# Loads issued from two hardware queues instead of one, in a NaN-ignoring row maximum

## The chip, the cores and the metric

The kernel runs on one core of a Trainium2 chip. The metric is the device time of the whole program in microseconds (us). Every run told here was of the fast state: executions of one kernel agree within 0.3% for the kernel before, and within about 1% for most of the kernels with late loads that follow. Ratios are the mean time of one kernel's fast runs over the mean of the other's in the same rounds on the same chip, so they are not quite the ratios of the medians that are quoted.

## The reference

```python
def setup_inputs():
    batch, seq, dim = 32, 2048, 2048
    x = np.random.randn(batch, seq, dim).astype(np.float32)
    mask = np.random.rand(batch, seq, dim) < 0.1
    x[mask] = np.nan
    return {"x": x, "axis": -1}

def reference(x, axis):
    return np.nanmax(x, axis=axis).astype(np.float32)
```

The input is 537 MB and each element is needed once; the output is 0.26 MB.

## The kernel before

Each of the 128 partitions takes its share of the 65,536 rows. A tile holds seven rows of 2048 floats per partition, 7 MB in all, and there are three tile buffers. ScalarE turns the upper half of each float into a 16-bit key in which NaN sorts low (a "piece" of two or three rows), GpSimd turns the key back and writes it into the tile, and VectorE takes the maximum. Once in three tiles ScalarE itself does the turning back for the last piece, to relieve GpSimd; this is called the write-back here. A negative number in the piece list marks it.

```python
TILES = (
    [([1], [1], [1])]
    + [
        ([7], [2, 3, 2], [2, 3, 2]),      # loads, pieces, reduces
        ([7], [2, 3, 2], [2, 3, 2]),
        ([7], [2, 3, -2], [2, 3, 2]),     # -2: write-back by ScalarE
    ] * 19
    + ...                                 # cut: the last tiles, in smaller and smaller loads
)
...
    io = ctx.enter_context(tc.tile_pool(name="io", bufs=3))
    mid = ctx.enter_context(tc.tile_pool(name="mid", bufs=3))
...
        for loads, pieces, reds in g:
            xt = io.tile([P, WIDE * D], i32, tag="xt")
            at = 0
            for c in loads:
                nc.sync.dma_start(                       # every load on SyncE's queue
                    out=xt[:, at * D : (at + c) * D],
                    in_=xg[:, (base + at) * D : (base + at + c) * D],
                )
                at += c
            ...
            for c in pieces:
                ...
                nc.scalar.activation(out=kp, in_=xp.bitcast(i16)[:, 1::2], func=ACT.Prelu, ...)
                if back:
                    nc.scalar.activation(out=xp.bitcast(i16)[:, 1::2], in_=kp, func=ACT.Copy, ...)
                else:
                    nc.gpsimd.tensor_scalar(out=xp.bitcast(i16)[:, 1::2], in0=kp, ...)
                ...
                    nc.vector.tensor_reduce(out=acc[...], in_=xt[...], op=ALU.max, ...)
```

The program is written in the order of the data. A scheduler then decides the order in which the instructions of each engine stand, and puts in the waits. The order on ScalarE is the scheduler's, unless it is pinned.

Of the kernel before, what the change touches and what calls it, by code (L numbers as in the profile page):

```python
# [1 line left out]

# [4 lines left out]
# [9 lines that stand above are left out]
        ([7], [2, 3, -2], [2, 3, 2]),  # L17
    ] * 19
    + [([7], [2, 3, 2], [2, 3, 2])] * 2
    + [([1, 6], [-1, 3, 1, -2], [4, 3])]  # L20
    + [([7], [3, 2, -2], [3, 4])]
    + [([7], [2, 2, 3], [2, 2, 3])] * 2
    + [([7], [2, 1, 2, 2], [2, 1, 2, 2])]
    + [([5, 2], [1, 1, 1, 2, -1, 1], [1, 1, 1, 3, 1])]
    + [([3, 4], [2, -1, 2, 2], [3, 2, 2])] * 2
    + [([3, 4], [2, -1, 1, 1, 2], [3, 2, 2])]
    + [([3, 2, 2], [1, 2, 1, -1, 1, 1], [1, 4, 2])]
    + [([3, 2, 2], [2, 1, 1, -1, 1, 1], [2, 1, 2, 2])]
    + [([2, 1, 2, 2], [1, 1, 1, 1, -1, 1, 1], [2, 3, 1, 1])]
    + [([2, 1, 1, 1, 2], [1, 1, 1, 1, -1, 1, 1], [1, 1, 1, 2, 1, 1])]  # L30
    + [([1, 1, 1, 1, 1, 1, 1], [1, 1, 1, -1, 1, 1, -1], [1, 1, 2, 1, 1, 1])]
)

GROUPS = [TILES[:14]] + [TILES[i : i + 12] for i in range(14, 74, 12)]
WIDE = 7

KEYS = 3



TOP = 0x7F7F
NAN = 0x7FC0
LOW = -129

EDGE = TOP + 0.25

NONE = -255.0 * 2.0**120


@with_exitstack  # L50
def kernel(
    ctx: ExitStack,
    tc: tile.TileContext,
    x: bass.AP,
    axis: bass.AP,
    out: bass.AP,
):









    nc = tc.nc
    P = nc.NUM_PARTITIONS
    f32, i32 = mybir.dt.float32, mybir.dt.int32
    i16, u16 = mybir.dt.int16, mybir.dt.uint16  # L70
    ALU = mybir.AluOpType
    ACT = mybir.ActivationFunctionType

    nd = len(x.shape)
    assert axis in (-1, nd - 1), axis
    D = x.shape[-1]

    xr = x.bitcast(i32).flatten_outer_dims()
    R = xr.shape[0]
    of = out.bitcast(i32).flatten_outer_dims().rearrange("r c -> (r c)")  # L80
    rows = [sum(sum(loads) for loads, _, _ in g) for g in GROUPS]
    assert R == P * sum(rows)

    io = ctx.enter_context(tc.tile_pool(name="io", bufs=3))
    mid = ctx.enter_context(tc.tile_pool(name="mid", bufs=3))
    res = ctx.enter_context(tc.tile_pool(name="res", bufs=1))
    sing = ctx.enter_context(tc.tile_pool(name="sing", bufs=1))
    flag = ctx.enter_context(
        tc.tile_pool(name="flag", bufs=2, space=bass.MemoryType.PSUM)
    )  # L90
    top = sing.tile([P, 1], f32)
    nc.vector.memset(top, EDGE)  # L92
    warm = sing.tile([P, 1], f32)
    nc.scalar.activation(out=warm, in_=top, func=ACT.Prelu, alpha=0.5)  # L94

    stores = []
    used = KEYS
    r0 = 0
    for s, g in zip(rows, GROUPS):
        xg = xr[r0 : r0 + P * s].rearrange("(p s) d -> p (s d)", p=P)  # L100
        og = of[r0 : r0 + P * s].rearrange("(p s) -> p s", p=P)
        r0 += P * s
        acc = res.tile([P, s], f32, tag=f"acc{len(stores)}")
        base = 0
        for loads, pieces, reds in g:
            assert sum(loads) == sum(abs(c) for c in pieces) == sum(reds)
            xt = io.tile([P, WIDE * D], i32, tag="xt")
            at = 0
            for c in loads:
                nc.sync.dma_start(  # L110
                    out=xt[:, at * D : (at + c) * D],
                    in_=xg[:, (base + at) * D : (base + at + c) * D],
                )
                at += c
            at = done = 0
            reds = list(reds)
            for c in pieces:
                back, c = c < 0, abs(c)
                xp = xt[:, at * D : (at + c) * D]
                if used + c > KEYS:  # L120
                    kt = mid.tile([P, KEYS * D], u16, tag="kt")
                    used = 0
                kp = kt[:, used * D : (used + c) * D]
                used += c
                nc.scalar.activation(  # L125
                    out=kp,
                    in_=xp.bitcast(i16)[:, 1::2],
                    func=ACT.Prelu,
                    bias=top,
                    scale=-1.0,  # L130
                    alpha=float(TOP - LOW) / (EDGE - NAN),
                )
                if back:
                    nc.scalar.activation(  # L134
                        out=xp.bitcast(i16)[:, 1::2],
                        in_=kp,
                        func=ACT.Copy,
                        bias=float(TOP),
                        scale=-1.0,
                    )  # L140
                else:
                    nc.gpsimd.tensor_scalar(  # L142
                        out=xp.bitcast(i16)[:, 1::2],
                        in0=kp,
                        scalar1=-1.0,
                        scalar2=float(TOP),
                        op0=ALU.mult,
                        op1=ALU.add,
                    )
                at += c  # L150
                while reds and done + reds[0] <= at:
                    n = reds.pop(0)
                    nc.vector.tensor_reduce(  # L153
                        out=acc[:, base + done : base + done + n],
                        in_=xt[:, done * D : (done + n) * D]
                        .bitcast(f32)
                        .rearrange("p (c d) -> p c d", c=n),
                        axis=mybir.AxisListType.X,
                        op=ALU.max,
                    )  # L160
                    done += n
            base += at
        none = flag.tile([P, s], i32, tag="none")
        nc.vector.tensor_scalar(  # L164
            out=none,
            in0=acc,
            scalar1=NONE,
            scalar2=float(0x00C00000),
            op0=ALU.is_equal,
            op1=ALU.mult,  # L170
        )
        bits = acc.bitcast(i32)
        nc.vector.tensor_tensor(out=bits, in0=bits, in1=none, op=ALU.bitwise_or)  # L173
        stores.append(dict(out=og, in_=bits))
    for st in stores:
        nc.sync.dma_start(**st)


# [1 line left out]
_INS = ['x', 'axis']  # L180
_OUTS = [((32, 2048), 'float32')]

_NUMBERS = {'axis': -1}


# [26 lines left out]
```

## Time and profile before

In the profile lines DVE is VectorE, ACT is ScalarE, POOL is GpSimd; SPq and ACTq are the sequencers of SyncE and ScalarE, which read the engine's instructions in order and issue its loads. L125 is line 125 of the kernel; q1 is SyncE's DMA queue and q10 ScalarE's. A load has *landed* when its semaphore, the counter that other instructions wait for, says that all of it has arrived.

| | before |
|---|---|
| time, median of 3 runs | 1261.39 us (1261.24 to 1261.41) |
| span of the profiled run | 1259.5 us |
| share of the DMA engines' span that SyncE's queue takes | 98.9% |
| one 7 MB tile, landing to landing | 16.9 us |

From the page of before: busy times, the rows of 40 equal slices for the DMA engines (tenths busy, and GB/s moved), the queue table and the chain of work that ended last.

```profile
span 1259.5 us, 1258 instructions
DVE 1115.2 (89%) x242; ACT 1053.3 (84%) x281; POOL 1091.2 (87%) x219
...
DMA  9999999999999999999999999999999999999995
GB/s 412 437 437 437 437 424 421 437 438 437 435 433 435 417 435 437 437 435 435 435 426 424 437 437 434 435 435 436 419 433 437 433 438 435 420 432 429 427 425 214
...
q1 hardware_dynamic: 14688, 537.14, 98.9%
...
DMA 29%; POOL 27%; ACT 20%; issue 17%; DVE 7%; SPq 0%; ACTq 0%; POOLq 0%; DVEq 0%
```

The three compute engines are 84 to 89% busy, but the queue is busy 98.9% of the span. The chain of waits, with its 29% of DMA, does not show this at once: it walks through compute, as the load at its steps was let go by a reduce. The queue row does.

The timeline of before in the middle of the run (columns: start, duration, engine, line, operation, count, and in brackets the idle time before it with what ended it):

```profile
605.12 8.74 DVE L153 TENSOR_REDUCE acc<-xt 128x2 f32<-128x4096 f32 x2
609.56 17.15 SPq L110 DMA_DIRECT2D xt<-in_x_dram  x2
...
616.04 12.62 ACT L125 ACTIVATE kt<-xt,top 128x4096 uint16<-128x4096 int16 x3 [4.33 <-DMA xt<-in_x_dram]
628.69 4.76 ACT L134 ACTIVATE xt<-kt 128x4096 int16<-128x4096 uint16 x1
...
633.32 3.68 ACT L125 ACTIVATE kt<-xt,top 128x4096 uint16<-128x4096 int16 x1
```

The load at 609.56 goes out when VectorE is done with an old tile, 6.5 us before the tile ahead of it lands (616.04, where ScalarE begins). That distance is called the load's **lead**: the landing of the load ahead of it, less its own issue. In before the lead is 6 us or more in every one of the 58 large loads of the steady part. The write-back at 628.69 stands ahead of the next tile's first piece at 633.32.

What SyncE's sequencer waited for in before (waiter, what it waited for, total us, times, longest us):

```profile
SPq L110 <- DVE acc L153: 1072.0, 66, 27.0
```

SyncE has nothing else to do, so these 1072 us of waiting cost nothing.

### The profile page before, as it was taken

To read this page: it belongs to the slowest core of one execution; us is meant where nothing else is said; L and a number is where in the kernel's file an instruction comes from. 1 tells how busy PE (TensorE), PEld (TensorE's weight loads), DVE (VectorE), ACT (ScalarE), POOL (GpSimd) and SP (SyncE) were. 2 spreads that over 40 slices of the span, in tenths; PEclk is the share of its full clock that TensorE was granted. 3 is DMA by queue.
4 is the path that set the end of the run, shared out by engine and by line. 5 is a ranking of instruction groups with operands and counts; after the bars stand their busy time and mean duration, and the time that the engine had idled before them with its cause. 6 is when DMAs were issued, how large, how long until landed. Compare 5 with 4: busy or idle time off the path is not lost.

```text
span 1259.5 us, 1258 instructions
## 1 busy us (share of the span) xinstructions
DVE 1115.2 (89%) x242; ACT 1053.3 (84%) x281; POOL 1091.2 (87%) x219
## 2 busy tenths in 40 slices
DVE  0888898888899898888989888999888889999999
ACT  4788797887888878878888788797887899799997
POOL 2989989889898898898988989889889896999996
DMA  9999999999999999999999999999999999999995
GB/s 412 437 437 437 437 424 421 437 438 437 435 433 435 417 435 437 437 435 435 435 426 424 437 437 434 435 435 436 419 433 437 433 438 435 420 432 429 427 425 214
DMA packets 14697, 537.21 MB, mean 427 GB/s; under 512 B 2400, under 2 KB 2400, under 8 KB 2400
## 3 DMA queue, kind: packets, MB, share of 16 engines
q1 hardware_dynamic: 14688, 537.14, 98.9%
q14 instruction: 9, 0.07, 0.0%
HBM read 536.87 MB, written 0.26 MB: 426 GB/s over the span
## 4 chain that ended last, share of the span: by engine, by line
DMA 29%; POOL 27%; ACT 20%; issue 17%; DVE 7%; SPq 0%; ACTq 0%; POOLq 0%; DVEq 0%
DMA xt<-in_x_dram 29%; POOL xt L142 27%; ACT kt L125 16%; DVE acc L153 7%; ACT xt L134 4%; SPq L110 0%; DVE none L164 0%; DVE acc L173 0%; ACTq L125 0%; POOLq L142 0%; DVEq L153 0%; ACTq L134 0%
## 5 line engine op out<-in xcount | busy, mean ns | idle before, releaser
L153 DVE TENSOR_REDUCE acc<-xt 128x2 f32<-128x4096 f32 (+2 forms) x229 | 1112.6, 4916 | 140.0 <-POOL xt L142 140.0
L142 POOL TENSOR_SCALAR xt<-kt 128x4096 int16<-128x4096 uint16 (+2 forms) x215 | 1091.0, 5074 | 159.1 <-ACT kt L125 146.7
L125 ACT ACTIVATE kt<-xt,top 128x4096 uint16<-128x4096 int16 (+2 forms) x247 | 927.9, 3821 | 196.7 <-DMA xt<-in_x_dram 196.5
L134 ACT ACTIVATE xt<-kt 128x4096 int16<-128x4096 uint16 (+1 forms) x32 | 127.5, 3983 | 1.0
L94 ACT ACT_TABLE_LOAD x1 | 1.3, 1283 | 0.7 <-PEq L193 0.7
L164 DVE TENSOR_SCALAR none<-acc 128x84 int32<-128x84 f32 (+1 forms) x6 | 1.5, 251 | 0.2
L173 DVE TENSOR_TENSOR acc<-acc,none 128x84 int32<-128x84 int32 (+1 forms) x6 | 1.5, 243 | 0.2
L92 DVE MEMSET top<- 128x1 f32 x1 | 0.1, 59 | 0.8 <-PEq L193 0.8
L193 POOL MEMSET const-float32-0.0<- 128x1 f32 x1 | 0.1, 99 | 0.2 <-issue 0.2
L94 ACT ACTIVATE warm<-top 128x1 f32<-128x1 f32 x1 | 0.2, 203 | 0.0
L193 POOL MEMSET const-uint8-127<- 128x1 uint8 x1 | 0.1, 103 | 0.0
L193 POOL MEMSET const-bfloat16-1.0<- 128x1 bf16 x1 | 0.1, 102 | 0.0
L193 POOL MEMSET const-float32-1.0<- 128x1 f32 x1 | 0.1, 99 | 0.0
## 6 DMA issues: line engine op xcount, KB each, us to landing
xt<-in_x_dram SPq DMA_DIRECT2D x63, 7168.0 KB, 23.5
xt<-in_x_dram SPq DMA_DIRECT2D x10, 2048.0 KB, 25.3
xt<-in_x_dram SPq DMA_DIRECT2D x5, 3072.0 KB, 16.1
xt<-in_x_dram SPq DMA_DIRECT2D x13, 1024.0 KB, 23.2
xt<-in_x_dram SPq DMA_DIRECT2D x3, 4096.0 KB, 25.1
xt<-in_x_dram SPq DMA_DIRECT2D x1, 6144.0 KB, 23.3
xt<-in_x_dram SPq DMA_DIRECT2D x1, 5120.0 KB, 18.5
out_dram<-acc SPq DMA_DIRECT2D x5, 42.0 KB, 10.7
```

The source lines that it names most:

```text
L92: nc.vector.memset(top, EDGE)
L94: nc.scalar.activation(out=warm, in_=top, func=ACT.Prelu, alpha=0.5)
L125: nc.scalar.activation(out=kp, in_=xp.bitcast(i16)[:, 1::2], func=ACT.Prelu, bias=top, scale=-1.0, alpha=float(TOP - LOW) / (EDGE - NAN),)
L134: nc.scalar.activation(out=xp.bitcast(i16)[:, 1::2], in_=kp, func=ACT.Copy, bias=float(TOP), scale=-1.0,)
L142: nc.gpsimd.tensor_scalar(out=xp.bitcast(i16)[:, 1::2], in0=kp, scalar1=-1.0, scalar2=float(TOP), op0=ALU.mult, op1=ALU.add,)
L153: nc.vector.tensor_reduce(out=acc[:, base + done : base + done + n], in_=xt[:, done * D : (done + n) * D] .bitcast(f32) .rearrange("p (c d ...
L164: nc.vector.tensor_scalar(out=none, in0=acc, scalar1=NONE, scalar2=float(0x00C00000), op0=ALU.is_equal, op1=ALU.mult,)
L173: nc.vector.tensor_tensor(out=bits, in0=bits, in1=none, op=ALU.bitwise_or)
L193: nc = _bacc.Bacc("TRN2", target_bir_lowering=False, num_devices=1)
```

## The change

Its intent: issue whole-tile loads in turn from SyncE's and ScalarE's queues, two tiles ahead of the work, so that two transfers can be in flight from two issuers.

```diff
+    ahead = []
+    ...                                   # cut: the list of all tiles' loads
+    ready = []
+    queues = [nc.sync, nc.scalar]
+
+    def fetch():
+        xg, base, loads = ahead.pop(0)
+        xt = io.tile([P, WIDE * D], i32, tag="xt")
+        queue = queues[0]
+        if len(loads) == 1:
+            queues.reverse()
+        at = 0
+        for c in loads:
+            queue.dma_start(
+                out=xt[:, at * D : (at + c) * D],
+                in_=xg[:, (base + at) * D : (base + at + c) * D],
+            )
+            at += c
+        ready.append(xt)
...
         for loads, pieces, reds in g:
-            xt = io.tile([P, WIDE * D], i32, tag="xt")
-            at = 0
-            for c in loads:
-                nc.sync.dma_start(...)
-                at += c
+            while len(ready) < 3 and ahead:
+                fetch()
+            xt = ready.pop(0)
```

Buffers, bytes and compute are the same. In the built program 32 loads stand in ScalarE's instruction stream. Over six tiles, with T8 to T13 as the example, that stream reads (L11 is the load of tile 11):

```
T8 p1 p2 p3 | T9 p1 p2 p3 | T10 p1 | L11 | T9 write-back | T10 p2 p3 | T11 p1 p2 p3 | L13 |
T12 p1 p2 p3 | T13 p1 | T12 write-back | T13 p2 p3 | L15 | ...
```

The scheduler has also moved the write-back behind the next tile's first piece.

More of the change, by code (lines that the diff above doesn't have):

```diff
@@ L94 @@
     nc.scalar.activation(out=warm, in_=top, func=ACT.Prelu, alpha=0.5)
+    ahead = []
+    r0 = 0
+    for s, g in zip(rows, GROUPS):
+        xg = xr[r0 : r0 + P * s].rearrange("(p s) d -> p (s d)", p=P)
+        r0 += P * s
+        base = 0
+        for loads, _, _ in g:
+            ahead.append((xg, base, loads))
+            base += sum(loads)
+    ready = []
[14 more added lines that the diff above has]
+        ready.append(xt)
     stores = []
@@ L99 @@
     for s, g in zip(rows, GROUPS):
-        xg = xr[r0 : r0 + P * s].rearrange("(p s) d -> p (s d)", p=P)
         og = of[r0 : r0 + P * s].rearrange("(p s) -> p s", p=P)
@@ L106 @@
             assert sum(loads) == sum(abs(c) for c in pieces) == sum(reds)
-            xt = io.tile([P, WIDE * D], i32, tag="xt")
-            at = 0
-            for c in loads:
-                nc.sync.dma_start(
-                    out=xt[:, at * D : (at + c) * D],
-                    in_=xg[:, (base + at) * D : (base + at + c) * D],
-                )
-                at += c
+            while len(ready) < 3 and ahead:
+                fetch()
+            xt = ready.pop(0)
             at = done = 0
```

## The prediction

> **What bounds it now.** The loads. The queue table of the page gives SyncE's queue 98.9% of the 16 DMA engines' span. A 7 MB tile takes 16.8 us at the 437 GB/s of the undisturbed slices. Engines have slack per 16.8 us tile (busy times of the page over 73 full tiles' worth): VectorE 15.2, GpSimd 14.9, ScalarE 14.4. By the timeline at 599-616 us, the load of tile n+2 is issued at 609.6, when VectorE has finished tile n-1 (three buffers), 10.5 us after ScalarE began tile n and 6.5 us before tile n+1 lands. So there is always a transfer behind the current one. A fresh load costs about 2.3 us besides its transfer (first load: 4.7 us from issue to landing, 2.4 of them transfer). The ceiling of any better issue is small: 1261 less 1229 of transfer, 3 at the start and about 15 at the end leaves some 12 us, 1%.
>
> **What changes.** Bytes, compute and buffers stay; 32 of the loads move to ScalarE's stream. "Two tiles ahead" is not new: SyncE already stood at the next free buffer. The Trainium skill ("DMA: Bandwidth & Descriptors", Issuing engines are not separate DMA queues) says that both queues run on the same 16 engines and interleave; the trace agrees in that one queue already fills them. Issue itself is 0.33 us on SyncE's sequencer: nothing to save.
>
> What it adds is order. SyncE's sequencer stood idle until the buffer came free; ScalarE's reaches a load only after the ScalarE instructions ahead of it have had their waits. In the trace a semaphore instruction of ScalarE's sequencer fires at once when the previous ACTIVATE's wait is met, even if that ACTIVATE starts 4.6 us later, so a load stands behind waits, not behind execution. The built order repeats every six tiles, three ScalarE loads:
> - one behind the first piece of the next tile, so issued only when that tile has landed and the DMA engines have nothing left: idle 2.4 us;
> - one behind a whole tile: on time;
> - one behind another tile's three pieces and behind a delayed write-back; that write-back (4.77 us on ScalarE) now stands after the next tile's first piece, so VectorE frees that buffer 5 to 9 us late. The same delay hits the SyncE load after it.
>
> Walking six tiles by hand with durations of the trace (ScalarE 3.70/5.40/4.77, GpSimd 4.77/7.04, VectorE 4.41/6.55, DMA 16.8+2.3 us, both queues sharing equally) gives idle DMA of about 2.4+0.4+0.7+2.3 us: a period of 106.5 instead of 101 us. Ten such periods: +56 us. Start (first tile shares with the second, the third load waits behind it) and end: +3 us. Stores issued earlier save nothing: the last one closes the chain. All of it is on the critical path, as the DMA bounds.
>
> **Predicted: 1320 us, range 1292 to 1352.** Faster by over 2%: 0.01; within 2%: 0.10; slower: 0.89.
>
> **Right if** the DMA row shows gaps of 2 to 3 us repeating every six tiles (mean 400 to 415 GB/s, queues' sum about 94%), two queues of similar share; mean durations of ACTIVATE, TENSOR_SCALAR and TENSOR_REDUCE unchanged; ScalarE's idle time before L147's pieces for DMA grows; SyncE waits for VectorE as before; ScalarE's queue shows waits for VectorE. The chain of waits gets a larger DMA share.
>
> **Wrong if** ScalarE's sequencer does stall until the ACTIVATEs ahead have executed: then the first load of each period is 3.7 us later, the third 4.4 us, and the time is nearer 1385. Or if sharing lets the older load finish first or if the engines' slack closes the gaps: then under 1286. If two queues moved more than 437 GB/s together, it would be faster; the trace gives no sign of it. Equal sharing by itself delays a landing but wastes no bandwidth, so it should not matter.

## The result, and the profile after

| | before | after |
|---|---|---|
| time, median of 4 runs | 1261.4 us | 1352.8 us (1348.07 to 1360.45) |
| ratio, 95% interval | | 1.073 (1.067 to 1.079) |
| span of the profiled run | 1259.5 us | 1346.5 us |
| queues' share of the DMA engines' span | 98.9% | 53.0% + 41.4% = 94.4% |

The change is 7.3% slower. The forecast of "slower" was right; 1352.8 lies just outside the range of 1292 to 1352, and the loss is 91 us where 59 were predicted.

The same parts of the page, after:

```profile
span 1346.5 us, 1217 instructions
DVE 1116.8 (83%) x242; ACT 1053.4 (78%) x281; POOL 1090.0 (81%) x219
...
DMA  9999999999999989999998999998999999899995
GB/s 413 436 395 424 404 378 422 414 372 421 392 382 400 426 370 374 426 402 385 409 385 356 434 429 390 382 434 356 407 412 407 376 414 434 350 428 428 428 427 236
...
q1 hardware_dynamic: 10080, 302.26, 53.0%
q10 hardware_dynamic: 4608, 234.88, 41.4%
...
DMA 53%; ACT 21%; DVE 11%; POOL 9%; issue 5%; SPq 0%; ACTq 0%; DVEq 0%
```

Busy times of the compute engines have not moved; the rate has fallen to 350 to 436 GB/s. The chain of waits is now 53% DMA.

The timeline of after, around one of the ScalarE loads that stand behind the next tile's first piece:

```profile
514.07 3.71 ACT L147 ACTIVATE kt<-xt,top 128x4096 uint16<-128x4096 int16 x1 [4.59 <-DMA xt<-in_x_dram]
514.10 0.33 ACTq L117 DMA_DIRECT2D xt<-in_x_dram  x1
...
517.69 4.75 ACT L156 ACTIVATE xt<-kt 128x4096 int16<-128x4096 uint16 x1
...
522.30 8.99 ACT L147 ACTIVATE kt<-xt,top 128x6144 uint16<-128x6144 int16 x2
...
532.54 0.33 SPq L117 DMA_DIRECT2D xt<-in_x_dram  x1
533.48 3.71 ACT L147 ACTIVATE kt<-xt,top 128x4096 uint16<-128x4096 int16 x1 [2.19 <-DMA xt<-in_x_dram]
```

The load goes out at 514.10, 0.03 us after the piece ahead of it has begun, that is, when the transfer ahead has just landed: its lead is about zero. The next tile lands at 533.4, 19.4 us after the last one instead of 16.9. The write-back stands at 517.69, behind the first piece, and the second piece waits for it until 522.30. Two things can be read here of the issuing sequencer. The load did not wait for the ACTIVATE to end at 517.78. The Trainium skill ("Perfetto Trace Analysis", DVE / Act Engine Instruction) says that a sequencer pushes such an instruction into a wait queue and goes on; this trace agrees as far as a load passes an ACTIVATE that executes. It does not pass an unmet wait. Here the landing is waited for by a semaphore instruction of ScalarE's own sequencer, which fired at 514.01; piece and load follow it. An ACTIVATE's own unmet wait holds the sequencer too: in before, the semaphore instruction of the write-back at 620.34, whose own wait had been met for 6.5 us, fired 0.03 us after the GpSimd update for which the piece ahead of it waits, while that piece began only at 624.96. So it was in all 19 write-backs of the steady part.

The busy time in the same stretches (columns: stretch, its length, busy time of VectorE, ScalarE and GpSimd, clock, DMA share, GB/s), two slow tiles of after and then two of before:

```profile
494.50:514.00 19.50, 18.39 (x7) 12.72 (x3) 19.26 (x4) 1.00 0.91 379
514.00:533.40 19.40, 16.88 (x4) 17.22 (x4) 13.64 (x3) 1.00 0.90 378
```

```profile
616.00:632.90 16.90, 15.28 (x4) 16.83 (x4) 16.11 (x3) 1.00 1.00 434
632.90:649.80 16.90, 14.94 (x4) 13.01 (x4) 12.10 (x3) 1.00 1.01 435
```

The waits of SyncE's sequencer after:

```profile
SPq L117 <- DVE acc L175: 973.3, 36, 37.9
```

SyncE, with half the loads, still waits for VectorE most of the time; the longest wait has grown from 27.0 to 37.9 us.

At the start, the first piece of ScalarE came at 23.19 us instead of 5.43, seen in these timeline lines of before and of after. The first tile, 8192-byte packets on SyncE's queue, took turns with 57344-byte packets of the second tile on ScalarE's.

```profile
5.43 2.00 ACT L125 ACTIVATE kt<-xt,top 128x2048 uint16<-128x2048 int16 x1 [3.20 <-DMA xt<-in_x_dram]
```

```profile
23.19 10.91 ACT L147 ACTIVATE kt<-xt,top 128x2048 uint16<-128x2048 int16 x3 [20.51 <-DMA xt<-in_x_dram]
```

The Trainium skill ("DMA: Bandwidth & Descriptors", Queues, rings and completion order) says that a DMA engine goes round-robin between queues, a whole packet at a time; this agrees. It was made good soon after: tile 4 landed only 0.9 us later than before.

### Where the time went

Two pieces of arithmetic on the page. DMA time is share times span: before 98.9% of 1259.5 = 1245.6 us, after 94.4% of 1346.5 = 1271.1 us. So of the 87 us by which the span grew, **61.5 us is DMA engines without a packet** (13.9 before, 75.4 after) and **25.5 us is packets that take longer**, for the same bytes.

In the packet records most 57344-byte packets take 2.12 us in both kernels. Of the 606 after that take over 2.3 us, 584 are among the first sixteen packets of a load, which are the first on each of the 16 DMA engines where these had run dry: for the load at 514.10, thirteen of the sixteen first packets took 2.60 to 3.00 us.

Averages over eight repeats of the six-tile pattern after (tiles 12 to 59), worked out from each load's issue and landing (the time at which its semaphore is full); "excess" is the time between landings over the 16.94 us of before:

```
load                                             lead us   excess us   predicted idle us
ScalarE, behind the next tile's first piece       -0.1       2.74        2.4
next three (SyncE, ScalarE, SyncE) together        1.4*      1.93        0.4 + 0 + 0
ScalarE, behind three pieces and a write-back      0.4       2.35        0.7
SyncE, the one after it                            0.8       1.88        2.3
sum                                                          8.90        5.8
* of the first of the three; the other two have leads over 8 us
```

What held these loads back is not the same for all. The first of the table stands behind a wait in ScalarE's stream: in all eight repeats its own buffer had been free for 2.7 to 3.1 us. The other late ones, the second one on ScalarE included, went out within 0.07 us of the reduce that freed their buffer. They are late because VectorE is, which waits for the moved write-back; the lines before the load at 475.71, of the third row, show it:

```profile
466.48 4.74 ACT L156 ACTIVATE xt<-kt 128x4096 int16<-128x4096 uint16 x1
...
471.26 8.74 DVE L175 TENSOR_REDUCE acc<-xt 128x2 f32<-128x4096 f32 x2 [2.61 <-ACT xt L156]
475.71 0.33 ACTq L117 DMA_DIRECT2D xt<-in_x_dram  x1
```

Of the 8.9 us, 2.7 fall on the load that ScalarE's stream holds and 6.2 on those that VectorE's reduces hold. Each late landing also makes VectorE later, so this says where the time shows, not how much each of the two causes is worth alone.

### The profile page after: what moved, and what is told of

Its sections match the earlier page's. It is cut to its first block, busy times and chain, and to the rows that moved or that the text cites. A ratio compares the mean times of both kernels' runs of the same rounds, so it can differ in the third digit from the quotient of the medians.

```text
span 1346.5 us, 1217 instructions
## 1 busy us (share of the span) xinstructions
DVE 1116.8 (83%) x242; ACT 1053.4 (78%) x281; POOL 1090.0 (81%) x219
## 3 DMA queue, kind: packets, MB, share of 16 engines
q10 hardware_dynamic: 4608, 234.88, 41.4%
## 4 chain that ended last, share of the span: by engine, by line
DMA 53%; ACT 21%; DVE 11%; POOL 9%; issue 5%; SPq 0%; ACTq 0%; DVEq 0%
DMA xt<-in_x_dram 53%; ACT kt L147 17%; DVE acc L175 11%; POOL xt L164 9%; ACT xt L156 4%; SPq L117 0%; ACTq L147 0%; DVE acc L195 0%; DVE none L186 0%; ACTq L117 0%; DVEq L175 0%
```

## The experiments

Theory A: what counts is the lead of each load, and loads come late because they stand behind unmet waits in ScalarE's stream or because the write-back was moved. Theory B: two queues that share the DMA engines cost something by themselves. Rival C: a load in a compute engine's stream costs, as its wait blocks the engine. Theory D: where two queues share the end of a load, its completion is told late, and that lag is the missing 30 us. All runs gave correct results.

| run | median us | ratio to before (95%) | over before, us |
|---|---|---|---|
| rewritten fetch, SyncE alone | 1261.29 | 1.000 (0.998 to 1.002) | 0 |
| two queues, timely loads | 1288.4 | 1.022 (1.019 to 1.026) | 27 |
| same, one load in six late | 1322.99 | 1.049 (1.047 to 1.051) | 62 |
| all loads on ScalarE | 1342.19 | 1.064 (1.061 to 1.067) | 81 |
| before, small packets (control) | 1275.74 | 1.011 (1.010 to 1.013) | 14 |
| after, small packets | 1368.33 | 1.084 (1.081 to 1.087) | 107 |
| timely, small packets | 1295.71 | 1.027 (1.024 to 1.030) | 34 |
| timely, load ahead of the write-back | 1270.27 | 1.007 (1.005 to 1.009) | 9 |
| SyncE alone, load only after the last landing | 1408.53 | 1.117 (1.115 to 1.118) | 147 |
| SyncE alone, loads some 4 us late | 1312.68 | 1.040 (1.039 to 1.042) | 51 |
| SyncE alone, write-back late | 1300.03 | 1.031 (1.029 to 1.032) | 39 |

### The rewritten fetch on one queue

```diff
-    queues = [nc.sync, nc.scalar]
+    queues = [nc.sync, nc.sync]
```

> The changed kernel with both entries of its queue list set to SyncE: the rewritten fetch stays, ScalarE's stream holds no load. Theory A (the loss is load issues that come too late because they stand behind waits in ScalarE's stream): back to 1261 us, within 5. Theory B (two hardware queues that share the DMA engines cost bandwidth or delay landings, whatever the issue times): also about 1261. If the rewritten fetch itself were at fault: 1340 or more.

Measured 1261.29 us, as before. The rewritten loop is not at fault, nor "two tiles ahead": three buffers already allowed that.

### Two queues, timely loads

ScalarE's own instructions and the loads are pinned to the order of the program, and the fetch moves to the end of its tile.

```diff
-            while len(ready) < 3 and ahead:
+            while not stores and not base and len(ready) < 3:   # the first three only
                 fetch()
             xt = ready.pop(0)
...
-                nc.scalar.activation(...)
+                tc.keep_in_program_order(nc.scalar.activation(...))   # pieces, write-backs; loads too
...
+            while len(ready) < 2 and ahead:
+                fetch()
             base += at
```

> Two queues as in the change, but ScalarE's stream is pinned: each ScalarE load stands right behind its tile's own pieces, the write-back stays ahead of the next tile's first piece. A load is then issued about 10.5 to 12.6 us after its tile's start, 4 us before the transfer in flight ends. Theory A: 1261 to 1272 us, DMA row without gaps, queues' sum above 97%. Theory B: most of the loss stays, 1320 us or more. Landing lag of a load that shares its end with the other queue (2.5 us where it is 0.45 alone) should be seen in nearly every load under both; under A it costs little as the issue slack covers it.

Measured 1288.4 us: most of the loss is gone, but this is above the 1272 that theory A had allowed. In its trace 38 of the 58 large loads landed 2.5 us after their last packet, and 19 had a lead under 4.5 us. Two readings were left: the lag (theory D), or leads that are still too short.

### One load in six late

```diff
-            while len(ready) < 2 and ahead:
+            k = n_tiles - len(ahead)
+            while len(ready) < 2 and ahead and not (k % 6 == 5 and k < 63):
                 fetch()
...
             # in the loop over pieces, behind a piece's own instructions
+                if len(ready) < 1 and ahead:
+                    fetch()
```

> As the run with timely loads, but one load in six (the ten of tiles 5, 11, ... 59) is put behind the first piece of the tile before it, as the changed kernel has it; the write-backs stay on time. Theory A: each costs the 2.5 us that the trace of after shows for such a load (19.4 us between landings where 16.94 is the transfer), so about 25 us over the timely run: 1283 to 1300 us. Theory B: same as the timely run within 8 us.

Measured 1322.99 us, 35 us more than the timely run for ten late loads, 3.5 us each, where 2.5 were expected; it lies above the expected range. The late load is costly, and it shortens others: 34 loads had a lead under 4.5 us instead of 19.

### All loads on ScalarE

```diff
-    queues = [nc.sync, nc.scalar]
+    queues = [nc.scalar, nc.scalar]
```

> Both entries of the queue list set to ScalarE: one queue, every load in ScalarE's stream, where the scheduler put each behind the second piece of its tile with a wait for VectorE. Theory A: issue at about 10.5 to 13 us after the tile's start, still ahead of the end of the transfer in flight, so 1261 to 1280 us in spite of 60 and more loads in that stream. A rival C, that a load in a compute engine's stream costs by itself (its wait blocks ScalarE): above 1330. Theory B expects no loss, as one queue shares with nobody.

Measured 1342.19 us, a clear miss of the expectation, and it has one queue, so theory B has nothing to say here. Its group of two-row pieces shows a new wait (busy us, mean ns, then idle time before them and what ended it):

```profile
L147 ACT ACTIVATE kt<-xt,top 128x4096 uint16<-128x4096 int16 x139 | 510.5, 3700 | 239.0 <-DVE acc L175 201.8 <-DMA xt<-in_x_dram 36.8 <-issue 0.3
```

ScalarE waits 202 us for VectorE. It never needs anything of VectorE there: the load that stands ahead of the piece does, and the piece waits behind the load. So rival C holds a part. By tile 59 the run is 39 us behind before; 41 of 58 loads have leads of 2 to 4.5 us, none of them near zero. The other 43 us arise at the end: the last load, one of the small ones, lands 64 us later than before, and the program ends 82 us later.

This run corrected the theory, since here, on one queue, loads with a lead of 2 to 4.5 us lost time. The prediction had held 2.3 us to be enough.

### Small packets: control, after, and timely

A row of 57344 bytes is cut into four packets of 14336. The order of ScalarE's and VectorE's instructions in the second of the three is that of the changed kernel.

```diff
                 in_=xg[:, (base + at) * D : (base + at + c) * D],
+                max_dma_last_dim=7 * D if c == 7 else None,
             )
```

> Control for the next two: the kernel before with each 57344-byte row of the 7 MB loads cut into four DMA packets of 14336 bytes. The loads at the kernel's end, which have 16384-byte rows already, take 17.1 us per 7 MB where the large rows take 16.94, so about 1261 to 1275 us.

> The changed kernel with the same packets of 14336 bytes; every engine's order is that of the changed kernel. Theory D (where two queues share the end of a load, its completion is told one packet of the other queue late: 2.5 us from last packet to landing instead of 0.45): the lag falls to about 0.9 us in the 20 to 30 loads that have it and the time over its control falls from 91 us to 55 to 75 us, so 1320 to 1345. If the lag does not matter: 91 us over its control, 1352 to 1365.

> The run with timely loads (27 us over before, 38 of its loads landing 2.5 us after their last packet) with packets of 14336 bytes. Theory D: the lag shrinks to about 0.9 us, which gives the leads back that it had taken, so within 10 us of the control. If something else of the two queues costs: 20 us or more over the control.

The control measured 1275.74 us. The changed kernel with small packets measured 1368.33, 93 us over its control, where the changed kernel is 91 us over before. The lag did fall as meant (over 1 us in 11 loads instead of 20, and 1.0 us there instead of 2.5), and nothing came of it; 37 loads had a lead under 4.5 us in both. The timely run with small packets is 20 us over its control, where theory D allowed 10. Theory D falls.

### Timely, with the load ahead of the write-back

```diff
                 # edit of the timely run, behind a tile's last piece
+                if len(ready) < 2 and ahead and at + c == WIDE and k0 < 64:
+                    fetch()
                 if back:
                     pin(nc.scalar.activation(   # the write-back
```

> The run with timely loads, 57344-byte packets again, but in the tiles with a write-back the ScalarE load stands ahead of the write-back, not behind it, so it is issued at 10.5 us after its tile's start instead of 12.7. In the run with all loads on ScalarE a load lost nothing if issued more than 4.5 us before the transfer ahead of it landed, and 0.7 us at 4.0 to 4.5, 1.3 at 2 to 3.5. So 2.1 us more lead is worth most of the loss: 1262 to 1275 us. If lateness is not what is left of the timely run's loss: 1280 to 1295.

Measured 1270.27 us, inside the expectation of theory A. Two queues, 32 loads in ScalarE's stream, 52 of 58 loads with the 2.5 us lag, and yet only 9 us over before: 6 loads had a lead under 4.5 us. The trace says where these are lost: tile 12 lands 11.3 us later than before and tile 59 9.7 us, so the loss lies in the first loads (the lead is -1.7 us at tile 4 and 2.35 to 3.2 at tiles 5, 6, 9 and 10), and nothing is lost after them. So in the steady part neither a second queue nor ScalarE's stream costs anything by itself, if the loads are on time. The timely runs undo both causes, the load behind an unmet wait and the moved write-back; they do not split the 91 us between them. Nor does either gain anything, as theory and the queue's 98.9% had said.

### Late loads on the old queue: after the landing

The kernel before, with one wait added on SyncE.

```diff
-                nc.sync.dma_start(...)
+                ld = nc.sync.dma_start(...)
+                lds.append(ld)
+                if 4 < len(lds) <= 60:
+                    tc.add_manual_dep(ld.ins, lds[-2].ins.name, ...)   # wait for the load ahead
```

> The kernel before, all loads on SyncE, with one more wait: each of the 56 loads of tiles 4 to 59 waits until the load ahead of it has landed, as one load in six of the changed kernel does. No second queue and nothing new in ScalarE's stream. Theory A (a load's lead over the landing ahead of it is all that counts): each costs what such loads cost in the trace of after, 2.73 us between landings, of which 0.7 us is in the first packet on each DMA engine (2.6 to 3.0 us instead of 2.12), so 1261 + 56 x 2.73 = 1414 us, 1400 to 1430; packet time per load 17.6 us instead of 16.97. Were a fresh load to cost 2.3 us, as the prediction had it: 1390. Theory B (two queues, ScalarE): near 1261.

Measured 1408.53 us, 147 us over before for 56 loads. Its page:

```profile
span 1407.4 us, 1257 instructions
...
GB/s 421 391 365 391 365 391 365 369 365 386 394 365 365 365 378 396 375 365 365 376 400 363 373 367 365 391 365 365 366 391 390 359 392 441 427 432 431 425 427 244
...
q1 hardware_dynamic: 14688, 537.14, 91.2%
```

A fresh load costs 2.68 us between landings here, with no second queue anywhere: 0.67 us of it in longer packets (17.64 us of packet time for a load instead of 16.97), about 2 us in empty DMA engines.

### Late loads on the old queue: about 4 us late

```diff
+                if len(firsts) > 3 and len(firsts) < 63:
+                    tc.add_manual_dep(ld.ins, firsts[-2].ins.name, ...)   # a tile's first reduce
```

> The kernel before, all loads on SyncE, each load of tiles 4 to 62 made to wait for the first reduce of the tile two before it: issued about 14.9 us after that tile's landing instead of 10.5. The lead falls from 6.5 to 2 us plus whatever is lost, so about 3. From the run with all loads on ScalarE (1.3 us lost at a lead of 2 to 3.5) 59 loads lose 1.25 us each: 1335 us, 1305 to 1350. By the prediction's own rule, that a lead over 2.3 us loses nothing: 1261 to 1275.

Measured 1312.68 us, within the expected range. A lead of about 4 us (median 3.9) still loses; by the prediction's rule nothing should have been lost. From this run and the one before it, loads of one queue, sorted by lead:

```
lead us        loads   packet time over 16.97   time between landings over 16.94
about 0          56             0.67                      2.68     (after the landing)
2.0 to 3.0        5             0.59                      1.75     (4 us late)
3.0 to 4.0       27             0.62                      1.07
4.0 to 4.5       14             0.52                      0.68
4.5 to 5.5       11             0.22                      0.06
over 5.5         58             0.00                      0.03     (before)
```

One load of the 4-us-late run, which comes behind small loads with a lead of -3.4 us, is left out. The lead counts to the landing, which is the end of the slowest DMA engine, and in the late runs the engines no longer end together. Counted from the packet records, the packets in flight first fell under 16 on average 2.6 us ahead of the landing in the 4-us-late run (54 of its loads), 1.1 us in the run after the landing, and in before hardly ever (2 of 56 loads). So part of a lead is used up before the landing. It is the smaller part: empty engines make 0.28 us a load in the 4-us-late run, the longer packets about 0.5.

### The late write-back on the old queue

The kernel before, ScalarE pinned, with the write-back and the reduce behind it emitted after the next tile's first piece.

```diff
                 if back:
-                    nc.scalar.activation(...)        # write-back
+                    held.append(write_back)          # run after the next tile's first piece
...
+                while held:
+                    held.pop(0)()
```

> The kernel before, all loads on SyncE, with only the write-back of the changed order: it and the reduce behind it stand after the next tile's first piece, once in three tiles. The buffer of that tile comes free at about 12.9 instead of 10.5 us after the landing, and the next tile's pieces are 4.8 us late, so two loads in three tiles have a lead of about 4 instead of 6.5 us: 0.7 us each, 38 loads, 1275 to 1300 us. By the prediction's rule of 2.3 us: 1261 to 1266.

Measured 1300.03 us, at the upper end of what theory A allowed. Moving one instruction of 4.75 us in three tiles behind one of 3.7 us costs 39 us in a kernel whose ScalarE is 84% busy: the median lead falls from 6.6 to 4.0 us. The prediction had named this delay but its rule gave it little weight.

## Why the prediction was right or wrong

- *"What bounds it now: the loads", "nothing to gain"*: right. No run was faster than before; two queues done well were 0.7% slower.
- *The direction and the mechanism, loads that come late*: right, and shown. The same two queues with loads on time cost 9 us instead of 91; SyncE alone with late loads costs 51 to 147. Of the two causes that the prediction names, the wait in ScalarE's stream holds one load in six; the other late ones wait for VectorE behind the moved write-back, which alone cost 39 us on SyncE's queue. How the 91 us divide is not shown.
- *"A load stands behind waits, not behind execution"*: right; the load at 514.10 passed an ACTIVATE that ran until 517.78. So the named alternative of 1385 us did not come.
- *"Equal sharing ... should not matter"*: right; from tile 12 to 59 the best two-queue run lost nothing. The lag of 2.5 us that it brings was not foreseen, and the runs with small packets show that it is not the cause.
- *"Mean 400 to 415 GB/s, queues' sum about 94%"*: 399 and 94.4%. *"Start ... and end: +3 us"*: the start cost 0.9 us at tile 4; the end added about 7 (last landing 86.5 us later than before, tile 59 79.9).
- **The step that failed is the cost of a late load: "A fresh load costs about 2.3 us besides its transfer", and its use in the walk, where a load issued 2.3 us ahead lost nothing.** That figure came from one 1 MB load at the start. The sum that it fed was "2.4+0.4+0.7+2.3" us in six tiles; measured were 2.74, 1.93, 2.35 and 1.88, that is 8.9 instead of 5.8. The walk's 0.4 and 0.7 were what 2.3 leaves of leads a little under 2 us, but at 2 to 3 us of lead a load still loses 1.75, and nothing is free below about 4.5. The late-load runs on the old queue show this without the change's queues or order. Some of the leads came out otherwise than in the walk, too, but the smaller part lies there: put into the prediction's own rule (2.3 less the lead), the measured leads give 6.7. In the profiled run, 87 us over before where 59 were predicted, the loads from tile 4 to 59 cost 79 us instead of 56, start and end 8 instead of 3.
- The sum of idle DMA time was predicted well (59 us of loss in all; 61.5 us of added idle measured), in part by luck: counted from the packets in flight, the four terms measured about 2.1, 0.7, 2.2 and 1.1 us where 2.4, 0.4, 0.7 and 2.3 were predicted, so that two large errors cancel. The missing 25.5 us are packets that take longer, for which the prediction had no term. A share of busy time cannot show them: they count as busy, so 94% was "confirmed" while the time was wrong.
- The range was also too narrow at the top for an estimate resting on one such figure.

What stays open: why the first packets of a load are longer even at a lead of 4 us, when an idle DMA engine starts on a load 0.97 us after its issue (as that at 514.10); what makes the first loads of the best two-queue run late; and the 43 us at the end of the run with all loads on ScalarE.

## What to carry to other kernels

When DMA bounds a kernel, read the lead of each load, the time from its issue to the landing of the load ahead, and keep it above what a test shows to be free (4.5 us here); the fixed cost of one load (2.3 us here) was too small a guide. A load put into a compute engine's stream inherits every unmet wait ahead of it and lends its own wait to whatever stands behind it, so look at the built order, and at what else the scheduler moved, before believing in a second queue. If a queue's share is the proof, check the time per packet too: late loads make packets longer, and that counts as busy.

## What the Trainium skill lacked or had wrong

- "DMA: Bandwidth & Descriptors", Issuing engines are not separate DMA queues, says that issuing from several engines saves only issue time. The runs agree that it gains nothing (1270.27 us at best against 1261.4). The page lacks that it can cost 7.3%, because the loads stand in the other engine's stream behind its waits and the scheduler moved that engine's work.
- The same page, Anatomy of one DMA, fits a fixed cost of about 2.0 us plus bytes at 436 GB/s (measured there on the software path), which for 7 MB gives an estimate of 18.8 us. A load issued at the landing of the one before took 19.6 us (16.94 + 2.68), and the page has no figure for how early a load must be issued to lose nothing: about 4.5 us here, with 1.1 us lost at 3 to 4.
- The same page lacks that the first packet on each DMA engine of a late load is longer: 2.6 to 3.0 us instead of 2.12, 0.7 us per 7 MB load.
- The same page, Queues, rings and completion order, has the packet-wise turns; it lacks a figure for what they do to completion. A load that shared its end with another queue landed 2.5 us after its last packet with 57344-byte packets and 1.0 us with 14336-byte ones, against 0.47 alone; and a first tile of small packets landed with the large one beside it, at 23.2 instead of 5.4 us.
- The same page, Specifications, gives about 358 GB/s as the HBM limit per core; the table lacks the condition, given elsewhere in the skill, that both cores of a pair are at work. This core, running alone, read 437 GB/s in the undisturbed slices; the page's 435 GB/s for the fabric fits within 0.5%.
- "Perfetto Trace Analysis" lacks that ScalarE's sequencer does not go on past an ACTIVATE whose own wait is unmet: in the kernel before, its next instruction fired 0.03 us after the update that the ACTIVATE ahead waited for, 19 times of 19.
